# Layer 1's recurrence: TensorE in the order of the code, three items advanced stage by stage, state and systems stored compactly by head

## The chip, the cores and the metric

One core of one Trainium2 chip runs the whole program in one launch. The metric is device time in microseconds (us). Five engines work side by side, each through its own instructions in a fixed order: TensorE (PE; its weight loads are shown as PEld), VectorE (DVE), ScalarE (ACT), GpSimd (POOL), and SyncE (SP), which here only issues DMAs.

## The reference

One inference step of a two-layer trunk. Layer 0 is a gated delta rule, layer 1 is RWKV-7 time mixing; both run over 16 meta tokens and 1024 prompt tokens (one sequence) and over 8 decode sequences of 8 tokens. The change touches layer 1 alone. Its core, for 16 heads of width 64:

```python
def step(S, inp):
    r_t, k_t, v_t, d_t, kk_t, b_t = inp
    S = (S * d_t[:, :, None, :]
         + jnp.einsum('bhvk,bhk->bhv', S, -kk_t)[..., None] * b_t[:, :, None, :]
         + v_t[..., None] * k_t[:, :, None, :])
    return S, jnp.einsum('bhvk,bhk->bhv', S, r_t)
...
y = (y - mean) * lax.rsqrt(var + GN_EPS) * lnx_w.reshape(H, N) + lnx_b.reshape(H, N)
y = y + jnp.sum(r_h * k_h * r_k, -1, keepdims=True) * v_h
y = y.reshape(B, T, D) * jax.nn.silu(z)
return y @ w_o, S, xn[:, -1]
```

Everything is float32; the kernel computes the large dense products as sums of three products of split float32r parts.

## The kernel before, in words

The tokens lie in three segments (`SEGS`: 384, 384 and 336 columns). The first 64 columns are the 8 decode sequences, the rest the prompt. An item is a pair of heads `p` (8 of them) in a segment `s`: 24 items, each with six chunks `ci` of 64 tokens. The recurrence is evaluated in chunked form. A chunk's step needs the state `S` that the same pair left behind, so the six steps of an item, and the three items of a pair, are a chain; different pairs are independent.

For each item `rwkv_front` loads keys, decays and values and makes the decayed operands `AR` and `BK`, the score matrices `G` (matmuls `fG`), the transposed keys `BT` (`fBT`) and values `UV` (`fVT`) and the bonus term (`fbonus`, `rbv`); names with `f` in front are its PSUM tiles. `rwkv_step` does one chunk in a PSUM tile `rA` (`pA` in the code, one bank, three buffers). The two heads' state is kept as a block-diagonal 128x128 tile, so that one matmul serves both heads. In order: `AR` times state plus scores, a scaled copy `rX` on ACT for each head, the triangular system `rTT` times `rX`, a copy `UV` on ACT, `AR` times state again plus the scores of the outputs, `BT` times `UV`, the new state `rS` on DVE for each head, a copy `y` on ACT. `pre` is the decayed old state. `rwkv_finish` normalises `y` (`bnst`, `mv`, `grs`), transposes it (`zyT`) and gates it (`lz`, `yh`, `yl`). For segment 0 `rwkv_sample_read` and `rwkv_sample_write` handle the decode states (`drsr`, `drsw`, with masked operands `ue`).

Dense products run beside the recurrence: the gates of segments 1 and 2 (`zz`, 384 matmuls, weights `rwkv_w_rkvz`) and the output projection (`d`, 576 matmuls, weights `rwkv_w_o`), then the final norm (`finish`, `dfin`). A counter `tau` runs over the code that writes all this: item `n` starts its steps at `tau = 2n`, so three items are under way at once. A list scheduler with a model of times turns the code into the fixed order of every engine, TensorE's too.

Of the kernel before, what the change touches and what calls it, by code (L numbers as in the profile page):

```python
# [35 lines left out]
class Builder:  # L36
# [38 lines left out]
    def mm(self, out, lhsT, rhs, start=True, stop=True):  # L75
        self.nc.tensor.matmul(out, lhsT, rhs, start=start, stop=stop)  # L76

# [942 lines left out]
    def rwkv_gates(self, xa, s, pool, xb=None):  # L1020
# [3 lines left out]
        c0, n = SEGS[s]  # L1024
        for k in range(8):
# [5 lines left out]
            self.split(x, f[:, 0, k, 0:n], f[:, 1, k, 0:n], eng_lo="dve" if k % 2 else "pool")  # L1031
        xh, xl = ([f[:, x, k, 0:n] for k in range(8)] for x in (0, 1))
        for k in range(8):
            w = self.load_w(self.i["rwkv_w_rkvz"][0, 3][:, 128 * k:128 * k + 128])
            p = self.ps("d", 4, "z") if s == 0 else self.ps("z", 1, "z")
            c = 0
            for q in range(8):
                wh, wl = w[0][q // 4][:, q % 4], w[1][q // 4][:, q % 4]
                for l, r in ((wh, xh[q]), (wl, xh[q]), (wh, xl[q])):
                    self.mm(p[:, 0:n], l, r, start=c == 0, stop=c == 23)  # L1040
                    c += 1
            z = t(pool, [128, 384], "ev", 3) if s == 0 else t(pool, [128, 384], "zst", 2)
# [273 lines left out]
    def rwkv_front(self, p, s):  # L1316
        nc, t, ap, col = self.nc, self.t, self.ap, self.pcol
        P = Ctx()
        P.n = 8 * s + p
        NB = self.NB  # L1320
        pc = lambda n: col[n][:, p:p + 1]
        P.TT = t(ap, [128, 6, 64], "rTT", 3)
        nc.sync.dma_start(P.TT.rearrange("p c k -> p (c k)"), self.ttd[P.n])
# [6 lines left out]
        AR = P.AR = t(ap, [128, 6, 2, 64], "AR", NB)  # L1330
# [15 lines left out]
        bp = self.ps("f", 2, "bonus")  # L1346
        ph, pl = t(ap, [128, 384], "prh", 1, F32R), t(ap, [128, 384], "prl", 1, F32R)
        self.split(pr, ph, pl, "act", "pool")
        self.mm(bp[:, 0:384], self.bones, ph, start=True, stop=False)
        self.mm(bp[:, 0:384], self.bones, pl, start=False, stop=True)  # L1350
        bv = P.bv = t(ap, [128, 384], "rbv", NB + 1)
        nc.vector.tensor_tensor(bv, ld["v"], bp[:, 0:384], op=ALU.mult)

        G = P.G = t(ap, [128, 6, 2, 128], "G", NB)
        for c in (0, 3):
            for h in (0, 1):
                gp = self.ps("f", 2, "G")
                q = slice(64 * h, 64 * h + 64)
                for u in range(3):
                    self.mm(gp[:, 128 * u:128 * u + 128], flat(BK[q, c + u]), flat(AR[q, c + u]))  # L1360
                g3 = gp[:, 0:384].rearrange("p (q k) -> p q k", k=128)
                f = 0
                if s == 0 and c == 0:
                    nc.vector.tensor_tensor(G[:, 0, h, :], g3[:, 0, :], self.gms, op=ALU.mult)
                    f = 1
                nc.vector.tensor_tensor(G[:, c + f:c + 3, h, :], g3[:, f:3], self.gm.unsqueeze(1).broadcast_to([128, 3 - f, 128]),
                                        op=ALU.mult)
# [3 lines left out]
        for c in (0, 3):  # L1371
# [4 lines left out]
        vp = self.ps("f", 2, "VT")  # L1376
        for u in range(3):
            self.transpose(vp[:, 128 * u:128 * u + 128], ld["v"][:, 128 * u:128 * u + 128])
        for a in (0, 1):
            nc.scalar.copy(UV[0:64, a:6:2].rearrange("p c h k -> p c (h k)"),  # L1380
                           vp[64 * a:64 * a + 64, 0:384].rearrange("p (c k) -> p c k", k=128))
        return P

    def rwkv_step(self, p, s, P, ci):
        nc, t, ap = self.nc, self.t, self.ap
        AR, G, BT, UV, TT, DC = P.AR, P.G, P.BT, P.UV, P.TT, P.DC
        c = 6 * s + ci
        smp = c == 0
        if ci == 0:
            P.y = t(ap, [128, 3, 2, 64], "y", 4)  # L1390
        y = P.y[64 * (ci % 2):64 * (ci % 2) + 64, ci // 2]
        rk = self.rk2[:, 6 * P.n + ci:6 * P.n + ci + 1]
        hs = [slice(0, 64), slice(64, 128)]
        flat = lambda x: x.rearrange("p a b -> p (a b)")
        xs = P.xs if smp else None
        S = self.S[p]
        pA = self.ps("r", 3, "A")

        if c > 1:
            self.mm(pA[0:64, 0:128], AR[:, ci, 0], flat(S), start=True, stop=False)  # L1400
        for h in (0, 1):
            self.mm(pA[0:64, 64 * h:64 * h + 64], G[:, ci, h, 0:64], UV[:, ci, h, :], start=c <= 1, stop=c <= 1 or h == 1)
        X = self.X[P.n % len(self.X)]
        for h in (0, 1):
            src = pA[0:64, 64 * h:64 * h + 64]
            if smp:
                nc.vector.tensor_tensor(X[hs[h], h, :], src, xs[0:64, hs[h]], op=ALU.add)
                nc.vector.tensor_scalar(X[hs[h], h, :], X[hs[h], h, :], rk[hs[h]], None, op0=ALU.mult)
            else:
                self.act(X[hs[h], h, :], src, AF.Identity, scale=rk[hs[h]])  # L1410
        if c > 1:
            pre = t(ap, [128, 128], "pre", 3)
            self.act(pre, flat(S), AF.Identity, scale=DC[:, ci:ci + 1])
        self.mm(pA[64:128, 128:256], TT[:, ci, :], flat(X))
        self.act(UV[64:128, ci].rearrange("p h k -> p (h k)"), pA[64:128, 128:256], AF.Identity, scale=-1.0)
        if c > 1:
            self.mm(pA[64:128, 256:384], AR[:, ci, 1], flat(S), start=True, stop=False)
        for h in (0, 1):
            self.mm(pA[64:128, 256 + 64 * h:320 + 64 * h], G[:, ci, h, 64:128], UV[:, ci, h, :], start=c <= 1,
                    stop=c <= 1 or h == 1)  # L1420
        py = pA[64:128, 256:384]
        if smp:
            nc.vector.tensor_tensor(flat(y), py, xs[64:128, :], op=ALU.add)
            return
        for h in (0, 1):
            self.mm(pA[hs[h], 384:448], BT[:, ci, hs[h]], UV[:, ci, h, :])
        for h in (0, 1):
            dS = pA[hs[h], 384:448]
            if c == 1:
                nc.vector.tensor_scalar(S[hs[h], h, :], dS, DC[hs[h], ci:ci + 1], None, op0=ALU.mult)  # L1430
            else:
                nc.vector.scalar_tensor_tensor(S[hs[h], h, :], dS, DC[hs[h], ci:ci + 1], pre[hs[h], hs[h]], op0=ALU.mult,  # L1432
                                               op1=ALU.add)
        nc.scalar.copy(flat(y), py)

    def rwkv_finish(self, p, s, P):
# [8 lines left out]
        y6 = y.rearrange("p c h k -> p (c h) k")  # L1445
# [6 lines left out]
        yp = self.ps("z", 1, "yT")  # L1452
# [3 lines left out]
        for q in range(3):  # L1456
            self.transpose(yp[:, 128 * q:128 * q + 128], y[:, q].rearrange("p h k -> p (h k)"))
        t1 = t(ap, [128, 384], "t1", 1)
        nc.vector.scalar_tensor_tensor(t1[:, 0:n], yp[:, 0:n], self.lnw[:, p:p + 1], P.bv[:, 0:n], op0=ALU.mult, op1=ALU.add)
        nc.vector.scalar_tensor_tensor(zg[:, 0:n], t1[:, 0:n], self.lnb[:, p:p + 1], zg[:, 0:n], op0=ALU.add, op1=ALU.mult)  # L1460
        yh, yl = t(self.fin, [128, 384], "yh", 8, F32R), t(self.fin, [128, 384], "yl", 8, F32R)
        self.split(zg[:, 0:n], yh[:, 0:n], yl[:, 0:n])
        if s == 2:
            sp = self.ps("z", 1, "sT")
            S = self.S[p]
            self.transpose(sp[:, 0:128], S.rearrange("p h k -> p (h k)"))
            so = t(ap, [128, 64], "so", 1)
            for h in (0, 1):
                q = slice(64 * h, 64 * h + 64)
                nc.scalar.copy(so[q], sp[q, q])  # L1470
            nc.sync.dma_start(self.o["p_rwkv"][0, 0, 2 * p:2 * p + 2].rearrange("h v k -> (h v) k"), so)
        return yh, yl

    def rwkv_sample_read(self, p, P, AR):

        nc, t, ap = self.nc, self.t, self.ap
        st = self.i["state_rwkv"][0].rearrange("(g u) h v k -> u v g h k", u=2)
        sn = t(self.fin, [128, 4, 2, 64], "sn", 1)
        for u in (0, 1):
            for g in range(4):  # L1480
                nc.sync.dma_start(sn[64 * u:64 * u + 64, g], st[u][:, g, 2 * p:2 * p + 2, :])
        sp = self.ps("d", 2, "sn")
# [3 lines left out]
        nc.scalar.copy(P.Sb.rearrange("p b k -> p (b k)"), sp)  # L1486
        rp = self.ps("d", 2, "rsr")
# [6 lines left out]
        self.transpose(rp[:, 128:256], q.rearrange("p x b r -> p (x b r)"))  # L1494
        xs = t(ap, [128, 128], "xss", 3)
        nc.vector.tensor_copy(xs, rp[:, 128:256])
        return xs

    def rwkv_sample_write(self, p, P, BT, UV, DC):
        nc, t, ap = self.nc, self.t, self.ap  # L1500
        ps = self.ps("d", 2, "rsw")
        for h in (0, 1):
            ue = t(self.fin, [128, 8, 64], "ue", 2)
# [5 lines left out]
        nc.vector.tensor_tensor(P.Sb, P.Sb, DC[:, 6:14].unsqueeze(2).broadcast_to([128, 8, 64]), op=ALU.mult)  # L1509
        op = self.ps("d", 2, "sbT")  # L1510
# [10 lines left out]
    def project_out(self, s, yo, pairs, x2):  # L1521

        nc, t, i = self.nc, self.t, self.i
        c0, n = SEGS[s]
        for ft in range(8):
            w = self.load_w(i["rwkv_w_o"][0][128 * pairs[0]:128 * pairs[-1] + 128, ft * 128:(ft + 1) * 128], len(pairs))
            if len(x2) < 8:
                x = t(self.fin2, [128, 384], "x2", 8)
                nc.sync.dma_start(x[:, 0:n], self.x1T[ft][:, c0:c0 + n])
                x2.append(x)  # L1530
            x = x2[ft]
# [3 lines left out]
            for k, q in enumerate(pairs):  # L1535
                wh, wl = w[0][k // 4][:, k % 4, :], w[1][k // 4][:, k % 4, :]
# [245 lines left out]
```

## Time and profile before

| | |
|---|---|
| three runs | 2451.74, 2457.27, 2458.03 us; median 2457.27 |
| profiled execution | 2460.66 us, span 2458.9 us |
| TensorE busy | 2273.3 us, 92% of the span |
| DVE, ACT, POOL busy | 66%, 56%, 43% |
| first and last matmul of the recurrence | 1872.8 us and 2418.2 us |

The profile is of one execution. Busy time of TensorE is the union of its matmuls from start to modelled end, and since matmuls are pipelined, a busy TensorE can hold stalls of up to about one matmul's length. Every float32 matmul stands in the trace as two rows here, called passes below; float32r products and transposes are one row each.

### The profile page before, as it was taken

Reading aid. Unit: us, or ns where it says so; the run is one execution under the profiler, and the core shown is the slowest. Engines: PE = TensorE matmul, PEld = TensorE weight load, DVE = VectorE, ACT = ScalarE, POOL = GpSimd, SP = SyncE. Lnnn points to the kernel's source line nnn. Section 1 sums busy time; section 2 is a strip of 40 time slices with the busy share of each in tenths; the row PEclk is TensorE's granted clock in tenths of the full one; section 3 lists DMA queues with packets and bytes.
Section 4 is the critical chain, followed back from the end, with each engine's and each line's share of the span. In section 5 each row is a group of like instructions: output and inputs, shape, how many; then the busy total and the mean of one; then the engine's idle time right before and its main releaser. Section 6 shows DMA issues by size and latency. Waiting matters only on the chain. (4 is left out here: it accounts for less than half of the span.)

```text
span 2458.9 us, 52218 instructions
## 1 busy us (share of the span) xinstructions
PE 2273.3 (92%) x18377; PEld 2041.3 (83%) x18377; DVE 1632.2 (66%) x4338; ACT 1370.2 (56%) x3817; POOL 1061.1 (43%) x1454
## 2 busy tenths in 40 slices
PE   6989999999999999999999999998879998998996
PEld 5888989898988989889899998777768877877875
DVE  6868676876768586843358344798865586576554
ACT  5445546555555564664336466564434666677673
POOL 3435343433444343451315235343456554554543
PEclk9989999999999999999999999989989998999998
DMA  3323333333332424261531556667665552342331
GB/s 109 106 69 99 85 107 84 102 86 85 87 102 66 117 79 109 71 204 57 145 100 42 163 176 159 173 186 194 152 193 166 141 150 80 94 148 78 106 102 54
DMA packets 471935, 284.61 MB, mean 116 GB/s; under 512 B 187481, under 2 KB 457050, under 8 KB 471674
## 3 DMA queue, kind: packets, MB, share of 16 engines
q1 hardware_dynamic: 471674, 281.29, 40.6%
q8 instruction: 145, 2.38, 0.4%
q14 instruction: 116, 0.95, 0.1%
HBM read 200.00 MB, written 81.17 MB: 114 GB/s over the span
## 5 line engine op out<-in xcount | busy, mean ns | idle before, releaser
L86 POOL TENSOR_TENSOR wlo<-wraw,whi 128x512 fp32r<-128x512 f32 x260 | 346.2, 1335 | 358.8 <-ACT whi L82 327.7
L82 ACT CAST whi<-wraw 128x512 fp32r<-128x512 f32 x260 | 159.9, 617 | 152.2 <-PE dq L76 50.6
L76 PE MATMUL d<-xc,whi 128*128 128x384 f32 (+3 forms) x846 | 237.9, 338 | 2.1 <-ACT ev L1145 2.1
L406 DVE SCALAR_TENSOR_TENSOR cvy<-raw,cw,cvy 128x408 f32<-128x408 f32 (+2 forms) x288 | 178.1, 631 | 16.6 <-ACT cvy L62 14.8
L439 DVE TENSOR_TENSOR invtmp<-invA,invT 72x31 f32<-72x31 f32 (+31 forms) x403 | 165.7, 411 | 16.7 <-POOL invT L434 6.0
L441 DVE TENSOR_TENSOR invT<-invT,invtmp 72x31 f32<-72x31 f32 (+31 forms) x403 | 169.1, 420 | 6.4
L76 PEld LDWEIGHTS d<-xc,whi 128*128 128x128 f32 (+1 forms) x846 | 154.5, 190 | 9.8 <-issue 5.3
L76 PE MATMUL dz<-xc,whi 128*128 128x384 f32 (+1 forms) x480 | 149.6, 343 | 0.0
L76 PE MATMUL dv<-xc,whi 128*128 128x384 f32 (+1 forms) x480 | 146.7, 335 | 0.0
L76 PE MATMUL d<-xa,whi 128*128 128x384 f32 (+3 forms) x450 | 140.0, 344 | 4.2 <-ACT xa L82 2.5
L76 PE MATMUL dz<-xa,whi 128*128 128x384 f32 (+1 forms) x416 | 137.3, 352 | 3.6 <-ACT whi L82 3.0
L76 PE MATMUL d<-xc,wlo 128*128 128x384 f32 (+2 forms) x396 | 130.6, 340 | 0.0
L76 PE MATMUL rA<-rS,AR 128*64 128x128 f32 x512 | 108.1, 295 | 18.2 <-ACT UV L62 7.5
L855 POOL TENSOR_SCALAR Sb<-Sb,eglb 128x128 f32<-128x128 f32 x128 | 81.1, 651 | 86.2 <-DMA Sb<-in_state_gdn 37.7
L76 PE MATMUL rA<-UV,G 128*64 128x64 f32 x1152 | 114.8, 225 | 0.8 <-ACT UV L1380 0.8
L76 PEld LDWEIGHTS rA<-UV,G 128*64 128x64 f32 x1152 | 104.0, 140 | 5.4 <-issue 2.3
L76 PE MATMUL dv<-xa,whi 128*128 128x384 f32 (+1 forms) x288 | 99.9, 347 | 0.1
L62 ACT ACTIVATE rX<-rA,rk 64x64 f32<-64x64 f32 x272 | 83.6, 307 | 20.6 <-PE rA L76 14.9
L1432 DVE SCALAR_TENSOR_TENSOR rS<-rA,DC,pre 64x64 f32<-64x64 f32 x256 | 72.2, 282 | 32.6 <-PE rA L76 27.7
L76 PEld LDWEIGHTS d<-xa,whi 128*128 128x128 f32 (+1 forms) x450 | 84.2, 192 | 9.4 <-ACT xa L82 2.8
L76 PE MATMUL dz<-xa,wlo 128*128 128x384 f32 (+1 forms) x256 | 89.8, 351 | 2.1 <-POOL wlo L86 2.1
L76 PEld LDWEIGHTS dz<-xc,whi 128*128 128x128 f32 x480 | 89.8, 192 | 0.8
(505 smaller groups left out, 7412.4 us busy)
## 6 DMA issues: line engine op xcount, KB each, us to landing
wraw<-in_gdn_w_in SPq DMA_DIRECT2D x96, 256.0 KB
wraw<-in_rwkv_w_rkvz SPq DMA_DIRECT2D x96, 256.0 KB
Sb<-in_state_gdn SPq DMA_DIRECT2D x64, 256.0 KB
wraw<-in_rwkv_w_o SPq DMA_DIRECT2D x48, 256.0 KB
E<-drow SPq DMA_DIRECT2D x24, 384.0 KB
attn<-drow SPq DMA_DIRECT2D x24, 384.0 KB
wraw<-in_gdn_w_out SPq DMA_DIRECT2D x36, 256.0 KB
out_s_gdn<-Sb SPq DMA_DIRECT2D x32, 256.0 KB
```

What stands on the lines that cost most here:

```text
L62: return self.nc.scalar.activation(out, in_, func, bias=bias, scale=scale, **kw)
L76: self.nc.tensor.matmul(out, lhsT, rhs, start=start, stop=stop)
L82: nc.scalar.copy(hi, x)
L86: e.tensor_tensor(lo, x, hi.bitcast(F32), op=ALU.subtract)
L406: nc.vector.scalar_tensor_tensor(y[:, 0:wd], raw[:, k:k + wd], cw[k], y[:, 0:wd], op0=ALU.mult, op1=ALU.add)
L439: nc.vector.tensor_tensor(tmp, A[:, j, j + 1:32].unsqueeze(2).broadcast_to([nb, n, m]), Tv[:, j, 0:m].unsqueeze(1).broadcast_to([nb, n, m] ...
L441: nc.vector.tensor_tensor(Tv[:, j + 1:32, 0:m], Tv[:, j + 1:32, 0:m], tmp, op=ALU.subtract)
L855: nc.gpsimd.tensor_scalar(Sb[:, u], Sb[:, u], self.eglb[:, hv, 4 * g + u:4 * g + u + 1], None, op0=ALU.mult)
L1432: nc.vector.scalar_tensor_tensor(S[hs[h], h, :], dS, DC[hs[h], ci:ci + 1], pre[hs[h], hs[h]], op0=ALU.mult, op1=ALU.add)
```

## The change

State and systems: `S` becomes 128x64 (each head's 64x64 block on its own partitions), `X` becomes 128x64, and the systems `TT` are read into a tile that has zeros where the other head's rows would be. Products with the state are then one matmul for each head, 64 rows by 64 columns; all outputs of a step lie at the partitions of their head. One ACT copy makes `X` for both heads, one DVE instruction the new state.

Order: TensorE's instructions now keep the order in which the code writes them; the other engines stay with the list scheduler. The step is cut in five methods, and in each `tau` all items do one stage before any does the next. Into three gaps of each `tau` the code puts a part of the coming item's front, a piece of six dense matmuls (two pieces where two dense jobs are open, three before the first step), and pieces of the decode work. The front of an item is written one `tau` earlier. Weights of the dense products are fetched one tile ahead. The output projection runs in halves of four pairs in every segment. The outputs of a step are written after the new state. `ue` has one buffer instead of two.

```diff
+    def mmx(self, out, lhsT, rhs, start=False):
+        self.nc.tensor.matmul(out, lhsT, rhs, start=start, stop=True, skip_group_check=True)
...
+        P.parts = [[sc(0, 0)], [sc(0, 1), bonus], [values], [lambda: keys(0), sc(3, 0)], [system, sc(3, 1)], [lambda: keys(3)]]
...
+    def step_solve(self, P, ci):
+        if c > 1:
+            for h in (0, 1):
+                self.mmx(pA[hs[h], 0:64], AR[hs[h], ci, 0], S[hs[h]], True)
+            for h in (0, 1):
+                self.mmx(pA[hs[h], 256:320], AR[hs[h], ci, 1], S[hs[h]])
+    def step_scores(self, P, ci):
+        for h in (0, 1):
+            self.mmx(pA[hs[h], 0:64], G[:, ci, h, 0:64], UV[:, ci, h, :], c <= 1)
...
+        with self.tc.high_priority():
+            self.act(X, pA[:, 0:64], AF.Identity, scale=rk)
+        if c > 1:
+            P.pre = t(ap, [128, 64], "pre", 3)
+            self.act(P.pre, S, AF.Identity, scale=P.DC[:, ci:ci + 1])
+    def step_inner(self, P, ci):
+        for h in (0, 1):
+            self.mmx(pA[64:128, 128 + 64 * h:192 + 64 * h], P.TT[:, h, ci], P.X)
+        with self.tc.high_priority():
+            self.act(UV[64:128, ci].rearrange("p h k -> p (h k)"), pA[64:128, 128:256], AF.Identity, scale=-1.0)
+    def step_state(self, P, ci):
         for h in (0, 1):
+            self.mmx(pA[hs[h], 384:448], BT[:, ci, hs[h]], UV[:, ci, h, :])
+        with self.tc.high_priority():
...
+                nc.vector.scalar_tensor_tensor(S, pA[:, 384:448], DC[:, ci:ci + 1], P.pre, op0=ALU.mult, op1=ALU.add)
+    def step_outputs(self, P, ci):
         for h in (0, 1):
+            self.mmx(pA[64 * h:64 * h + 64, 256:320], G[:, ci, h, 64:128], UV[:, ci, h, :])
...
+            nc.scalar.copy(P.y[:, ci], pA[:, 256:320])
...
-        for q in range(3):
-            self.transpose(yp[:, 128 * q:128 * q + 128], y[:, q].rearrange("p h k -> p (h k)"))
+        yield
+        yp = self.ps("f", 2, "yT")
+        for q in range(6):
+            for h in (0, 64):
+                self.mm(yp[h:h + 64, 64 * q:64 * q + 64], y[h:h + 64, q], self.ident[h:h + 64, h:h + 64])
...
-            ue = t(self.fin, [128, 8, 64], "ue", 2)
+            ue = t(self.fin, [128, 8, 64], "ue", 1)
...
+        with tc.manual_schedule(engines={mybir.EngineType.PE}):
+            self.wave(xa, stay, last, pool)
...
+        for tau in range(-3, 54):
+            if (tau + 3) % 2 == 0 and (tau + 3) // 2 < 24:
+                s, p = divmod((tau + 3) // 2, 8)
+                P[8 * s + p] = self.rwkv_front(p, s)
+            m = (tau + 2) // 2
+            parts = P[m].parts[3 * (tau % 2):3 * (tau % 2) + 3] if 0 <= m < 24 else [[], [], []]
+            items = [(P[n], tau - 2 * n) for n in range(max(0, (tau - 4) // 2), min(24, tau // 2 + 1)) if 0 <= tau - 2 * n < 6]
+            stages = (self.step_solve, self.step_scores), (self.step_inner,), (self.step_state, self.step_outputs)
+            for g in range(3):
+                for f in stages[g]:
+                    for x in items:
+                        f(*x)
+                for f in parts[g]:
+                    f()
...
+                fill(3 if tau < 0 else 1 + (len(todo) > 1))
```

Three places show how the orders differ. On TensorE before, in the middle of the recurrence: `rA_27586` and `rA_27604` are the PSUM tiles of two items' steps.

```order
L76 MATMUL rA_27604<-rS_4107_23024,AR_27069 64x128
L76 MATMUL rA_27604<-UV_4115_23032,G_27091 64x64 x2
L76 MATMUL fbonus_27656<-prh_27657,bones_23011 128x384
L76 MATMUL fbonus_27656<-prl_27658,bones_23011 128x384
L76 MATMUL rA_27586<-rS_4106_23023,AR_26762 64x128
L76 MATMUL rA_27586<-UV_4114_23031,G_26784 64x64 x2
L76 MATMUL rA_27586<-UV_4114_23031,BT_26805 64x64 x2
L76 MATMUL rA_27604<-rX_4111_23028,rTT_27048 64x128
```

One item's products stand between the other's, each item at another point of its step. The same engine in the changed kernel, at the end of one `tau`: the three items' products for the state (`BT`), then the three for the outputs (`G`). What an instruction waits for stands behind it.

```order
L80 MATMUL rA_26753<-UV_4110_23027,BT_25600 64x64 [waits Activation_49]
L80 MATMUL rA_26753<-UV_4110_23027,BT_25600 64x64
L80 MATMUL rA_26759<-UV_4111_23028,BT_25962 64x64 [waits Activation_49]
L80 MATMUL rA_26759<-UV_4111_23028,BT_25962 64x64
L80 MATMUL rA_26766<-UV_4112_23029,BT_26294 64x64 [waits Activation_49]
L80 MATMUL rA_26766<-UV_4112_23029,BT_26294 64x64
L80 MATMUL rA_26753<-UV_4110_23027,G_25599 64x64 [waits DVE_49]
L80 MATMUL rA_26753<-UV_4110_23027,G_25599 64x64
L80 MATMUL rA_26759<-UV_4111_23028,G_25961 64x64 [waits DVE_49]
L80 MATMUL rA_26759<-UV_4111_23028,G_25961 64x64
L80 MATMUL rA_26766<-UV_4112_23029,G_26293 64x64 [waits DVE_49]
L80 MATMUL rA_26766<-UV_4112_23029,G_26293 64x64
```

The outputs moved behind the state's products, and each item's outputs now wait for DVE, which reads the same PSUM tile for the new state. Before, the outputs came first.

On ACT, before: the two copies `rX` of an item, and what stands behind them until the next copy `UV`.

```order
L62 ACTIVATE rX_4111_23028<-rA_27604,rk_10_97 64x64 [waits PE_49]
L62 ACTIVATE rX_4111_23028<-rA_27604,rk_10_97 64x64
L62 ACTIVATE fDp_27923<-fldcs_27911 128x384 [waits DMAHW0_49,Pool_49]
L82 CAST yh_27275<-lz_27242 128x384 [waits DVE_49]
L62 ACTIVATE UV_4115_23032<-rA_27604 64x128 [waits PE_49]
```

On ACT in the changed kernel, in the `tau` shown above: the three items' copies `X` and `UV`.

```order
L62 ACTIVATE X_26754<-rA_26753,rk_10_97 128x64 [waits PE_49]
L62 ACTIVATE X_26760<-rA_26759,rk_10_97 128x64 [waits PE_49,Activation_49]
L86 CAST yh_26749<-lz_26414 128x384 [waits DVE_49]
L62 ACTIVATE k_4950_26857<-flda_26838,omka_23017,pcol_385 128x384 [waits DMAHW7_49]
L62 ACTIVATE X_26767<-rA_26766,rk_10_97 128x64 [waits PE_49,Activation_49]
L62 ACTIVATE UV_4110_23027<-rA_26753 64x128 [waits PE_49]
L62 ACTIVATE UV_4111_23028<-rA_26759 64x128 [waits PE_49]
L62 ACTIVATE UV_4112_23029<-rA_26766 64x128 [waits PE_49]
```

Six copies became three, and the third `X` stands behind two ACT instructions of other work.

On DVE, before, around the new state of the two items above.

```order
L1352 TENSOR_TENSOR rbv_27663<-fldv_27632,fbonus_27656 128x384 [waits DMAHW6_49,PE_49]
L1448 BN_AGGR mv_27552<-bnst_27551 128x2 [waits DVE_49]
L1565 SCALAR_TENSOR_TENSOR f2k_27906<-dfin_27881,frs_27895,fw_24737 128x512 [waits DMAHW7_49,DMAHW6_49]
L1448 BN_AGGR mv_27552<-bnst_27551 128x2 [waits DVE_49]
L1432 SCALAR_TENSOR_TENSOR rS_4106_23023<-rA_27586,DC_26760,pre_27592 64x64 [waits PE_49]
L1432 SCALAR_TENSOR_TENSOR rS_4106_23023<-rA_27586,DC_26760,pre_27592 64x64
L1432 SCALAR_TENSOR_TENSOR rS_4107_23024<-rA_27604,DC_27067,pre_27610 64x64 [waits PE_49,Activation_49]
L1432 SCALAR_TENSOR_TENSOR rS_4107_23024<-rA_27604,DC_27067,pre_27610 64x64
```

On DVE in the changed kernel, in the same `tau` as above.

```order
L1352 TENSOR_TENSOR k_4950_26857<-k_4950_26857,fldk_26836 128x384 [waits DMAHW0_49,Activation_49]
L106 SCALAR_TENSOR_TENSOR grs_26724<-gn_t_26726,grs_26724 128x6 [waits DVE_49]
L1356 TENSOR_TENSOR BK_26861<-k_4950_26857,fiD_26847 128x6x64 [waits DVE_49]
L1361 SCALAR_TENSOR_TENSOR pr_26864<-fldr_26840,pcol_385,k_4950_26857 128x384
L1384 TENSOR_TENSOR G_26607<-fG_26801,gm_22991 128x3x128 [waits PE_49]
L1370 TENSOR_TENSOR rbv_26606<-fldv_26578,fbonus_26806 128x384 [waits PE_49]
L1469 SCALAR_TENSOR_TENSOR rS_4102_23019<-rA_26753,DC_25579,pre_26775 128x64 [waits PE_49,Activation_49]
L1469 SCALAR_TENSOR_TENSOR rS_4103_23020<-rA_26759,DC_25941,pre_26780 128x64 [waits PE_49,Activation_49]
L1469 SCALAR_TENSOR_TENSOR rS_4104_23021<-rA_26766,DC_26273,pre_26785 128x64 [waits PE_49,Activation_49]
```

The new states went from two instructions for each item to one, three in a row, behind the front's work for the next item.

More of the change, by code (lines that the diff above doesn't have):

```diff
@@ L1354, in rwkv_front, with bonus @@
-        G = P.G = t(ap, [128, 6, 2, 128], "G", NB)
[L1355 to L1367, printed above, removed]
+        def bonus():
+            bp = self.ps("f", 2, "bonus")
+            self.mm(bp[:, 0:384], self.bones, ph, start=True, stop=False)
+            self.mm(bp[:, 0:384], self.bones, pl, start=False, stop=True)
+            nc.vector.tensor_tensor(bv, ld["v"], bp[:, 0:384], op=ALU.mult)
@@ L1421, in rwkv_step @@
[L1421 to L1433, printed above, removed]
@@ L1754, with wave_out @@
+    def wave_out(self, P, n, x2, todo):
+        s, p = divmod(n, 8)
+        next(P[n].done, None)
+        half = lambda a, b: [P[8 * s + q].out for q in range(a, b)]
+        if p % 4 == 3:
+            x2.setdefault(s, [])
+            todo.append(self.project_out(s, half(p - 3, p + 1), range(p - 3, p + 1), x2[s]))
+        if p == 7:
+            todo.append(self.finish(s, x2[s]))
 _INS = ["x_prompt", "x_sample", "state_gdn", "state_gdn_conv", "state_rwkv", "state_rwkv_shift", "meta_tokens", "norm_w",
```

245 lines of the change are left out of this document (134 added, 111 removed).

## The prediction

> **What bounds the kernel now.** I read the page first, then the stretch from the recurrence's first matmul (1872.8 us) to its last (2418.2 us), then who waits there, then the timeline of TensorE for the price of a pass.
>
> ```profile
> PE 2273.3 (92%) x18377; PEld 2041.3 (83%) x18377; DVE 1632.2 (66%) x4338; ACT 1370.2 (56%) x3817; POOL 1061.1 (43%) x1454
> core 0: us, PE busy (x) PEld busy (x) DVE busy (x) ACT busy (x) POOL busy (x), PEclk, DMA share, GB/s
> 1872.80:2418.20 545.40, 511.00 (x4488) 425.46 (x4488) 348.59 (x1061) 367.45 (x1031) 291.98 (x327) 0.97 0.39 113
> ```
>
> In 545.4 us TensorE is idle for 545.4 - 511.0 = 34.4 us only. DVE is busy for 64%, ACT for 67%, POOL for 54%. The stretch is bound by what TensorE has to issue, so each pass saved there is time saved, until a wait takes its place.
>
> ```profile
> start us, us, engine line op out<-in xcount [idle before <-releaser]
> 2103.65 0.43 PE L76 MATMUL rA<-rS,AR 128*64 128x128 f32 x2
> 2103.92 0.22 PE L76 MATMUL rA<-UV,G 128*64 128x64 f32 x1
> 2103.92 0.27 PE L76 MATMUL rA<-UV,BT 128*64 128x64 f32 x1
> 2103.97 0.22 PE L76 MATMUL rA<-UV,G 128*64 128x64 f32 x1
> 2104.03 0.22 PE L76 MATMUL rA<-UV,BT 128*64 128x64 f32 x1
> 2104.03 0.28 PE L76 MATMUL rA<-UV,G 128*64 128x64 f32 x2
> 2104.15 0.28 PE L76 MATMUL rA<-UV,BT 128*64 128x64 f32 x2
> 2104.26 0.39 PE L76 MATMUL rA<-rX,rTT 128*64 128x128 f32 x2
> 2104.58 0.93 PE L76 MATMUL fG<-AR,BK 64*128 64x128 f32 x6
> 2105.44 0.43 PE L76 MATMUL rA<-rS,AR 128*64 128x128 f32 x2
> ...
> 2011.27 1.11 PE L76 MATMUL drsr<-AR,Sb 64*64 64x16 f32 x32
> 2012.31 0.43 PE L76 MATMUL rA<-rS,AR 128*64 128x128 f32 x2
> ```
> ```profile
> L76 PE MATMUL rA<-UV,G x1152: 219/222/366, 1872.8 to 2418.1; 128*64 128x64 f32 x192
> L76 PE MATMUL rA<-UV,BT x544: 222/222/368, 1892.7 to 2418.2; 128*64 128x64 f32 x182
> L76 PE MATMUL rA<-rS,AR x512: 272/275/476, 1895.6 to 2417.8; 128*64 128x128 f32 x171
> L76 PE MATMUL rA<-rX,rTT x288: 272/273/477, 1880.8 to 2417.0; 128*64 128x128 f32 x144
> L76 PE MATMUL drsr<-AR,Sb x256: 206/206/286, 1843.4 to 2012.2; 64*64 64x16 f32 x128
> ```
>
> The first fence is the timeline (start, length of the group), the second the tile views (shortest, median and longest pass in ns). A group's length less one pass's, divided by the rest of the count, is the spacing. Passes of 128 columns: (0.39 - 0.273) / 1 = 0.11 us. Passes of 64 columns to the same partitions: (0.28 - 0.222) / 1 = 0.058 us. The step's eight passes of `G` and `BT` take 0.34 us (2103.92 to 2104.26): a pass that writes partitions 64 to 127 and one that writes 0 to 63 start together at 2103.92, and four passes have gone by 2104.03, 0.029 us each. The `drsr` products, 64 rows by 64 columns for either head, also run at (1.11 - 0.206) / 31 = 0.029 us. After a change of shape the first pass comes late: `rTT` to `fG` takes 0.32 us, 0.10 more than its two passes.
>
> **The change part by part.** *Passes of the recurrence.* Before, a step has six passes of 128 columns (0.66 us), eight at 0.34 us together and four scores at 0.058 (0.23 us): 1.23 us, over 144 steps and less what the 16 first steps lack, 169 us. After, a step has 20 passes that alternate between the two heads' partitions and four (`step_inner`) that all write 64 to 127: 20 x 0.029 + 4 x 0.058 = 0.81 us, in all 112 us. **-57 us.** The alternation of whole heads (two passes, then two) is that of `drsr` and of `G` and `BT`; without any overlap it would be 24 x 0.058 = 1.39 us a step.
>
> *Transposes of `y`*: 72 transposes of one pass (0.11 us) become 288 matmuls of two passes at 0.029: 8 against 17 us, **+9**.
>
> *Changes of shape*: counted over the stretch in the two orders, 451 before and 491 after, at 0.10 us for the late pass and about 0.05 for the one behind it: **+6** (0 to 10).
>
> *Outputs behind the state.* This is the new wait.
>
> ```profile
> L1432 DVE SCALAR_TENSOR_TENSOR rS<-rA,DC,pre 64x64 f32<-64x64 f32 x256 | 72.2, 282 | 32.6 <-PE rA L76 27.7 <-ACT y L1434 0.5 <-ACT yh L82 0.4
> ACT y L1434 <- DVE rS L1432: 35.1, 43, 3.1
> ```
>
> In the kernel before, the copy `y` on ACT waits for the new state on DVE (35.1 us, 43 times) though both only read the tile; that wait lay on ACT, beside TensorE's work. Now TensorE itself stands in it: an item's outputs wait until DVE has read the tile, and what is queued behind is the whole coming gap. From the first `BT` pass: 0.06 + 0.22 us to the end of an item's passes, three DVE instructions of 0.28, and the last item's four passes, 0.12: 1.25 us, where 24 passes unhindered take 24 x 0.029 = 0.70. That is 0.55 us at least, and DVE reaches each of the three through a semaphore, for which I add 0.1. DVE is 64% busy with instructions of 0.33 us on average (348.59 / 1061); another 0.16 us for finding it occupied gives 0.8 us. There are 47 such rounds: **+38** (20 to 60; 30 with DVE always free, 47 x 0.65).
>
> *`ue` with one buffer.*
>
> ```profile
> L1504 POOL TENSOR_TENSOR ue<-UV,bmask 128x512 f32<-128x512 f32 x8 | 10.8, 1354 | 8.4 <-ACT UV L62 8.4
> L1504 DVE TENSOR_TENSOR ue<-UV,bmask 128x512 f32<-128x512 f32 x8 | 6.8, 845 | 1.9 <-ACT UV L62 1.8
> L76 PE MATMUL drsw<-ue,BT 128*64 128x512 f32 x32 | 9.7, 609 | 0.0
> ```
>
> The second head's `ue` (0.845 us on DVE) can begin only when the first head's matmul (0.61 us) has read the one buffer, and TensorE waits in order: 1.3 us, 8 times, **+10** (5 to 12).
>
> *The other waits.* TensorE can no longer go round a late operand. What hides the copies is a front part and a dense piece in each gap.
>
> ```profile
> L62 ACT ACTIVATE rX<-rA,rk 64x64 f32<-64x64 f32 x272 | 83.6, 307 | 20.6 <-PE rA L76 14.9
> 2200.54 0.44 PE L76 MATMUL d<-yh,whi 128*128 128x384 f32 x1
> 2200.82 0.34 PE L76 MATMUL d<-yl,whi 128*128 128x384 f32 x1
> ...
> 2201.71 0.34 PE L76 MATMUL d<-yh,whi 128*128 128x384 f32 x1
> ```
>
> Three copies `X` in a row take 3 x 0.31 us, and the pass before them 0.22, 1.2 us; a gap holds six `fG` passes (0.86 us, above) and, where there is dense work, six dense matmuls (2200.54 to 2201.71, 1.17 us): 2.0 us, covered. Counting the pieces that the code hands out (41 of the gates and 80 of the projection left after the first step, one or two a gap), about 12 of 52 rounds have none. There the third gap (a transposed group and the next `solve`) is short by some 0.5 us, and the second by about as much: 12 x 1.1 = 13 us. Late operands of other kinds I put at 9 us. So the idle 34 us of before become 22: **-12** (-25 to +45).
>
> *Start and tail.* 138 instead of 96 gate matmuls now stand ahead of the first step; at 0.18 us (five matmuls from 2200.82 to 2201.71) that is 7 us less in the stretch, of which the start pays back half: **-3** (-8 to +4). The projection's last half and the final norm keep their 41 us (2418.2 to 2458.9).
>
> *Other engines.* 272 copies `rX` become 136 (-42 us on ACT), 256 states 128 (-36 us on DVE); the projection in halves adds 16 DVE additions. Neither engine is the bound; at nothing on the path. SP issues two DMAs for a system instead of one: nothing, as the code writes them a round ahead of their first use.
>
> Sum: -57 + 9 + 6 + 38 + 10 - 12 - 3 = -9 us on the profiled execution's 2460.66 us (span 2458.9). That execution is 3.4 us above the median of the three runs; the same -9 on the median 2457.27 gives **2448 us**. What a measurement here can tell from no change is about 0.3%, 7.4 us.
>
> On the pairs that share all rows and differ in their output partitions (scores, state, outputs): the row above has them start together. The Trainium skill (TensorE: Matmul & The Clock Gate, Part 3: Packing small matmuls — row/col tiling) says that a weight load overlaps a matmul in flight only where the two use different row groups; by that rule these passes would not overlap, and the sum would be that of the second rival. The trace at 2103.92 speaks against it.
>
> **The rivals.** *A. ScalarE and VectorE become what TensorE waits for (slower).* Both keep an order laid out by a model, and TensorE now cannot go round them.
>
> ```profile
> L62 ACT ACTIVATE k<-flda,omka,pcol 128x384 f32<-128x384 f32 x20 | 14.1, 704 | 6.8 <-DMA flda<-ad 6.6
> L82 ACT CAST yh<-lz 128x384 fp32r<-128x384 f32 x16 | 8.1, 509 | 3.7 <-DVE lz L1460 3.3 <-PE d L76 0.3
> L1345 DVE SCALAR_TENSOR_TENSOR pr<-fldr,pcol,k 128x384 f32<-128x384 f32 x21 | 14.9, 711 | 1.7 <-POOL prl L86 1.6
> L1340 DVE TENSOR_TENSOR BK<-k,fiD 128x384 f32<-128x384 f32 x21 | 14.4, 685 | 3.7 <-PE fBT L73 3.2 <-ACT fiD L62 0.4
> ```
>
> In the changed order ACT has `yh` and `k` (0.51 + 0.70 us) ahead of the third `X`, and DVE has `BK`, `pr`, one `G` and `rbv` ahead of the new states. In every second round that delays `step_inner` by about 0.8 us and the states by as much: 24 x 1.6 = 38 us over the forecast, at 2486 us. For it: ACT and DVE are at two thirds before, and the stretch would get shorter. Against: in rounds with dense pieces 1.17 us for each gap cover it. It decides from 0.17 us a round (9 / 52).
>
> *B. The column pairs don't overlap (slower).* 1696 passes of scores, state and outputs at 0.058 instead of 0.029 us: +49 us, 2497 us. Against it stands the row at 2103.92.
>
> *C. The waits fit in the gaps.* DVE takes the states at once (30 instead of 38 us) and only 10 of the 34 idle us stay: another -20 us, 2428 us. For it: in the stretch before, no wait of TensorE's own on the recurrence's operands sums to much.
>
> ```profile
> PE rA L76 <- ACT UV L62: 7.5, 11, 1.5
> PE rA L76 <- DVE rS L1432: 6.6, 15, 0.8
> 2060.00:2100.00 40.00, 34.97 (x235) 27.47 (x234) 20.70 (x58) 21.66 (x61) 13.81 (x19) 0.74 0.21 65
> ```
>
> *D. The clock.* From 2060 to 2100 us the granted clock is 0.74. More short waits could bring another such stretch; each loses about 0.26 x 40 = 10 us, two of them put the result at 2468 us.
>
> **How the numbers follow.** Forecast (2438 to 2460 us) 0.40; A 0.30; B 0.04; C 0.22; D 0.04. Faster by over 0.3% (below 2449.9) are C and a little over half of the forecast: 0.44; within 0.3% the rest of the forecast: 0.18; slower A, B and D: 0.38. The unknown costs are the wait for DVE (20 to 60) and the other waits; the range, 2418 to 2488 us, takes in C with the least of both and A, and leaves out B and the joint extremes. The forecast's own range is 2438 to 2460 us.
>
> **What would show it.** Right: `rA` passes of `BT` and `G` in threes, a spacing of 0.029 us in the timeline; about 0.7 to 0.9 us between the last `BT` and the last `G` start of a round; waits "PE rA <- DVE rS" near 30 to 40 us; the stretch from first to last `rA` near 536 us. Wrong: spacing of 0.058 us (B); waits of `rA` on ACT `X` or DVE `G` of over 20 us (A); a stretch under 520 us (C); a granted clock under 0.95 in it (D).

## The result: slower by 1.3%, where 0.4% faster was forecast

| | before | changed |
|---|---|---|
| median | 2455.02 us (2451.74 to 2458.03, 4 runs) | 2486.28 us (2484.87 to 2493.25, 4 runs) |
| profiled execution, span | 2460.66, 2458.9 us | 2484.87, 2483.2 us |
| first to last matmul of the recurrence | 1872.8 to 2418.2 = 545.4 us | 1880.6 to 2443.9 = 563.3 us |

The ratio is 1.0127 (95% interval 1.0101 to 1.0152), against a forecast of 2448 us in a range of 2418 to 2488. The span grew by 24.3 us: the recurrence starts 7.8 us later, takes 17.9 us more, and what follows it takes 1.4 us less (40.7 against 39.3). Of the later start, 3.2 us lie ahead of the first gate matmul (1824.9 and 1828.1 us), in code that the change leaves alone. One of the six runs of experiment 9 took 3018.1 us at a granted clock of 0.65; the ratio given there leaves it out, the median of the six does not.

The page's first part, and the row of that stretch (columns as in the prediction):

```profile
PE 2275.2 (92%) x19737; PEld 2038.0 (82%) x19737; DVE 1600.7 (64%) x4193; ACT 1293.6 (52%) x3673; POOL 1069.5 (43%) x1454
1880.60:2443.90 563.30, 505.26 (x5782) 414.94 (x5781) 316.98 (x928) 288.01 (x884) 293.88 (x323) 0.94 0.37 108
```

ScalarE lost 79 us of work in the stretch (367.45 to 288.01) and VectorE 32 (348.59 to 316.98), and it bought nothing: TensorE is the bound. Its own busy time fell by 5.7 us although 1294 passes were added, and its idle time rose from 34.4 to 58.0 us. The granted clock fell from 0.97 to 0.94: by its records TensorE ran at half speed for 27.3 us of the stretch before, for 68.3 us after.

The chain of waits on TensorE, from 1880 to 2440 us (what waited, for whom: us in all, times, longest):

```profile
PE rA L80 <- DVE rS L1469: 22.9, 47, 2.2
PE dfin L73 <- DVE f2k L1620: 11.0, 4, 4.1
PE drsw L76 <- DVE ue L1554: 10.7, 8, 2.6
PE d L76 <- POOL yl L90: 3.4, 2, 2.3
PE fbonus L76 <- DVE G L1384: 3.2, 2, 2.0
PE rA L80 <- ACT X L62: 2.3, 5, 0.9
```

The first and the third were in the forecast, at 38 and 10 us. The second was not: the final norm's transposes `dfin` now stand in the recurrence in the order of the code, and those of a tile wait until VectorE has read the one before. The fourth is a projection waiting for the low part of its operand, which GpSimd makes. The last two are what rival A lived on; together they are 5.5 us.

One of the longest waits for `rS`, in the timeline of TensorE and then of VectorE:

```profile
2198.11 0.57 PE L80 MATMUL rA<-UV,BT 128*64 128x64 f32 x12
2200.77 0.91 PE L80 MATMUL rA<-UV,G 128*64 128x64 f32 x12 [2.09 <-DVE rS L1469]
2201.61 0.90 PE L73 MATMUL fVT<-ident,fldv 128*128 128x128 f32 x3
```
```profile
2198.34 0.55 DVE L1384 TENSOR_TENSOR G<-fG,gm 128x384 f32<-128x384 f32 x1
2198.81 0.71 DVE L1356 TENSOR_TENSOR BK<-k,fiD 128x384 f32<-128x384 f32 x1
2199.45 0.60 DVE L1361 SCALAR_TENSOR_TENSOR pr<-fldr,pcol,k 128x384 f32<-128x384 f32 x1
2199.98 0.54 DVE L1370 TENSOR_TENSOR rbv<-fldv,fbonus 128x384 f32<-128x384 f32 x1
2200.44 0.66 DVE L1469 SCALAR_TENSOR_TENSOR rS<-rA,DC,pre 128x64 f32<-128x64 f32 x3
```

Twelve passes of `BT` take 0.57 us, (0.57 - 0.222) / 11 = 0.032 us each: the overlap of the column pairs is there, and rival B is out. Then TensorE stands still for 2.09 us, since VectorE has four instructions of the next item's front ahead of the new states. And the three transposes behind take 0.90 us, where three such take 0.55 us at full speed (shown below).

That half speed can be followed in windows laid on the grid of the clock's records, 3.41 us wide:

```profile
2176.26:2179.67 3.41, 0.00 (x0) 0.00 (x0) 1.53 (x7) 0.93 (x4) 0.55 (x1) 1.00 0.32 103
2179.67:2183.08 3.41, 3.35 (x32) 2.92 (x32) 1.38 (x4) 1.38 (x4) 0.66 (x1) 0.50 0.52 132
2183.08:2186.50 3.42, 1.93 (x23) 1.48 (x21) 2.61 (x6) 1.51 (x5) 2.46 (x5) 1.00 0.03 8
2186.50:2189.91 3.41, 3.09 (x20) 2.79 (x20) 1.60 (x5) 1.72 (x6) 0.00 (x0) 0.50 0.66 224
2196.74:2200.15 3.41, 1.94 (x21) 1.43 (x20) 3.34 (x8) 1.64 (x6) 2.01 (x2) 1.00 0.55 156
2200.15:2203.56 3.41, 2.37 (x27) 1.85 (x29) 1.52 (x8) 2.71 (x10) 1.00 (x1) 0.50 0.49 154
2213.80:2217.22 3.42, 3.42 (x57) 3.19 (x56) 2.02 (x8) 1.10 (x3) 2.80 (x3) 0.50 0.00 0
```

Behind the window and its width stands TensorE's busy time; the third number from the end is the clock. The windows in which TensorE was busy for 0.00, 1.93 and 1.94 of 3.41 us at full clock are each followed by one at half clock, and the last stay at half speed goes on for five windows (2200.1 to 2217.2 us). No dense matmul stands in these five windows.

### The profile page after: what moved, and what is told of

Its sections match the earlier page's. It is cut to its first block, busy times and chain, and to the rows that moved or that the text cites. A ratio compares the mean times of both kernels' runs of the same rounds, so it can differ in the third digit from the quotient of the medians.

```text
span 2483.2 us, 54705 instructions
## 1 busy us (share of the span) xinstructions
PE 2275.2 (92%) x19737; PEld 2038.0 (82%) x19737; DVE 1600.7 (64%) x4193; ACT 1293.6 (52%) x3673; POOL 1069.5 (43%) x1454
## 5 line engine op out<-in xcount | busy, mean ns | idle before, releaser
L1384 DVE TENSOR_TENSOR G<-fG,gm 128x384 f32<-128x384 f32 (+1 forms) x96 | 50.8, 530 | 89.4 <-PE fG L76 89.3
L76 PE MATMUL zz<-xa,whi 128*128 128x384 f32 (+1 forms) x256 | 80.1, 364 | 15.0 <-DVE zst L1054 10.1
L76 PE MATMUL fG<-AR,BK 64*128 64x128 f32 x576 | 93.6, 298 | 0.0
L76 PEld LDWEIGHTS dz<-xa,whi 128*128 128x128 f32 x416 | 81.9, 199 | 9.1 <-ACT whi L86 7.5
L76 PEld LDWEIGHTS dv<-xc,whi 128*128 128x128 f32 x480 | 88.5, 188 | 0.5 <-issue 0.4
```

## The experiments

The theory: TensorE's work did shrink as worked out, and four things used up what was gained: the outputs behind VectorE, the one `ue`, the norm's tiles, and half speed in rounds without dense work. The rival that runs through all tests: these waits are only places where a chain of an item's stages shows, and whatever is removed comes back elsewhere. Unless said otherwise each kernel is the changed one with one edit. The chips of these runs took 2462 us for the kernel before, so kernels are compared by their ratios to it, and a difference in ratio is turned into us with some 2455 us. The changed kernel counts as 1.0127; on the chip of experiments 7, 9 and 10 it was 1.0151, so 6 us between two sets of runs are no finding.

**1. Outputs ahead of the state.**

```diff
-stages = ..., (self.step_state, self.step_outputs)
+stages = ..., (self.step_outputs, self.step_state, self.step_copy)   # step_copy: the copy y alone
```

> One part undone: the outputs' matmuls stand ahead of the state's again, and the copy y on ACT behind the new state on DVE; all else as in the changed kernel (2486.3 us). Theory: TensorE's wait between the last BT and the first G (28.7 us by spacing, 23.3 us as listed for rS) goes, and with it half-speed stretches that begin in it (68 us at half speed in the recurrence, 27 before): 2446 to 2461 us, half-speed time under 50 us. Rival 1 (the wait is displaced: the same item's next solve waits for the state instead, since its chain sets the length of a round): 2478 us or more. Rival 2 (the clock has a cause of its own): 2457 to 2466 us, with half-speed time still near 68 us.

Measured: 2468.17 us, ratio 1.0014 (0.9994 to 1.0035): 0.0113 less, 28 us. By that ratio it is some 2458 us on the chip of the forecast, where the theory and rival 2 overlap. The stretch is 538.7 us.

```profile
1896.30:2435.00 538.70, 494.00 (x5782) 409.44 (x5781) 320.17 (x927) 282.33 (x884) 289.88 (x323) 0.93 0.39 112
PE rA L80 <- ACT y L1485: 9.1, 7, 3.3
PE rA L80 <- DVE rS L1469: 1.9, 1, 1.9
```

The wait for `rS` went from 22.9 to 1.9 us, and only a part of it came back, on the copy `y`. But the time at half speed stayed, at 71.7 us. So the wait costs 25 to 28 us, within the forecast's 20 to 60, and it is not by itself what sets the clock: there the theory was wrong, and the half-speed time came as rival 2 had it. Whether the clock has a cause of its own is what experiments 4 and 5 ask.

**2. Two `ue`.**

```diff
-ue = t(self.fin, [128, 8, 64], "ue", 1)
+ue = t(self.fin, [128, 8, 64], "ue", 2)      # and X in 3 buffers instead of 4
```

> One part undone: ue has two buffers again (X has three instead of four to make room); all else as in the changed kernel (2486.3 us). Theory: the second drsw matmul of a decode write no longer waits for VectorE (10.7 us listed, 16.4 us by spacing, in eight places): 2472 to 2478 us. Rival 1 (waits are displaced, since another chain sets the round): 2483 us or more.

Measured: 2485.0 us, ratio 1.0087 (1.0061 to 1.0114), 10 us less. The time itself lies where the rival put it, but on a chip 7 us slower for the kernel before; by the ratio it is some 2476 us, as the theory had it. The interval overlaps that of the changed kernel (1.0101 to 1.0152), so the runs alone hardly separate the two. The stretch of the profiled execution fell by 11.3 us to 552.0, and the wait of `drsw` is gone from the list, which now begins:

```profile
PE rA L80 <- DVE rS L1469: 28.5, 46, 2.3
PE dfin L73 <- DVE f2k L1620: 11.1, 4, 4.1
```

The wait for `rS` reads 28.5 us here and 22.9 in the changed kernel, so a part of what was removed may have come back in it.

**3. The norm's tiles apart.**

```diff
                     nc.sync.dma_start(yp[...], y[0:nr])
             yield
+            for _ in range(3 if s < 2 else 0):
+                yield
```

> One thing added: in segments 0 and 1 the final norm's three tiles stand three empty pieces apart in TensorE's order, so that the transposes dfin of a tile find the PSUM of the tile before it read; all else as in the changed kernel (2486.3 us). Theory: the wait of dfin for f2k (11.0 us listed, 8.5 by spacing, four places) goes: 2475 to 2481 us, and fewer half-speed pieces from 2174 to 2200 us. Rival 1 (waits are displaced; the empty pieces take cover away elsewhere): 2484 us or more.

Measured: 2479.85 us, ratio 1.0074 (1.0048 to 1.0099), 13 us less, as the theory had it; the stretch is 551.1 us. `dfin` is gone from the list, and a wait of 4.5 us in one place is new, of the transposes `fyT` for `y` on GpSimd.

**4. Dense pieces spread.**

```diff
-fill(3 if tau < 0 else 1 + (len(todo) > 1))
+fill(3 if tau < 0 else 1 if g < 2 else tau < 16 or len(todo) > 1)
```

> One thing changed: from the seventeenth round on the dense pieces are handed out one to each of a round's first two gaps (in the third gap only when two dense jobs are open), so that no round is without a piece; all else as in the changed kernel (2486.3 us). Theory (half speed begins in rounds that wait without dense work): half-speed time in the recurrence falls from 68 to under 40 us, the wait before the outputs stays near 25 us, 2466 to 2480 us. Rival 1 (a piece in each gap hides no more than two in half of them): 2483 to 2490 us. Rival 2 (the clock has a cause of its own): half-speed time near 68 us.

Measured: 2461.84 us, ratio 0.9999 (0.9983 to 1.0015): 31 us less, more than expected, from the order of the dense matmuls alone.

```profile
1888.70:2420.50 531.80, 488.75 (x5758) 399.26 (x5757) 312.38 (x926) 286.06 (x882) 289.48 (x321) 0.97 0.39 113
PE rA L80 <- DVE rS L1469: 24.3, 48, 1.8
```

The wait for the state is as long as ever, and half speed fell to 30.7 us, 38 less than in the changed kernel. In all twelve runs the mean clock of the whole program was 0.967 to 0.972, in the four of the changed kernel 0.958 to 0.961. If half the issue is lost at half speed (an estimate from the granted 0.50), some 19 of the 31 us are the clock. The rest fits the waits: TensorE's idle time in the stretch fell from 58.0 to 43.0 us, and in the lists `dfin` waits for 7.1 us instead of 11.0 and `drsw` for 8.0 instead of 10.7. The two shares were not separated by a run of their own, and 24 matmuls of the projection moved behind the stretch.

**5. Work added to keep TensorE busy.** In the 16 rounds with no dense job open:

```diff
+if f == self.step_outputs and not todo and tau > 12 and items:
+    w = self.ps("d", 2, "warm")
+    for q in range(8):
+        self.transpose(w[:, 0:128], self.ident)
```

> Work added: between the state's and the outputs' products of each of the 16 rounds that have no dense job open, eight transposes of a constant into a spare PSUM buffer that nobody reads (0.11 us each, 14 us of TensorE's issue in all); all else as in the changed kernel (2486.3 us). Theory (half speed follows rounds in which TensorE is busy for too small a part): the wait for VectorE there takes up some 10 of the 14 us, the half-speed time falls from 68 to under 45 us: 2470 to 2484 us. Rival (half speed has a cause of its own): half-speed time 60 us or more, 2487 to 2500 us.

Measured: 2485.8 us, ratio 1.0105 (1.008 to 1.013).

```profile
1890.70:2442.00 551.30, 504.43 (x5908) 415.01 (x5909) 317.29 (x928) 289.24 (x884) 293.48 (x323) 0.98 0.38 110
PE rA L80 <- DVE rS L1469: 16.6, 38, 1.2
```

With 14 us of useless work more, the stretch is 12 us shorter, and half speed fell from 68.3 to 27.3 us. That is one execution of each, but in all six runs the mean clock of the whole program was 0.964 to 0.966, above each of the changed kernel's four (0.958 to 0.961). So most of the half-speed time has no cause of its own: it follows how busy TensorE is. By the ratio the kernel is not measurably slower for that work (1.0105 against 1.0127 and, in another set of runs, 1.0151); the absolute time missed the 2470 to 2484 us by 2, on a chip 7 us slower for the kernel before.

**6. The list scheduler for TensorE.** `manual_schedule` taken away.

> One part undone: TensorE is given to the list scheduler again like the other engines; layout, stages and the code's order as in the changed kernel (2486.3 us). Theory (the layout saves TensorE some 46 us and the fixed order loses more than that in waits that it cannot go round): faster than before, ratio 0.975 to 0.995, half-speed time under 45 us. Rival (the order is not at fault: the outputs behind the state and one ue cost the same in any order): ratio 1.005 or more.

Measured: 2470.32 us, ratio 1.0042 (1.0018 to 1.0065): the theory's 0.975 to 0.995 fell. The rival's 1.005 lies in the interval, but its reason, the same waits in any order, does not hold either:

```profile
1871.70:2425.10 553.40, 525.90 (x5884) 426.82 (x5883) 326.72 (x937) 302.20 (x896) 305.03 (x333) 0.97 0.39 114
PE rA L80 <- ACT UV L62: 11.1, 9, 2.8
PE rA L80 <- DVE rS L1469: 7.1, 9, 1.9
PE rA L80 <- ACT y L1480: 4.4, 3, 2.8
```

The waits for `ue` and `f2k` are gone, that for `rS` is a third, half speed is down to 34.1 us. The stretch is 9.9 us shorter and begins 38.5 us after the first gate matmul instead of 52.5, so some 24 us were won where the theory wanted 43 at least. The waits don't hold the rest: TensorE is idle for 553.4 - 525.9 = 27.5 us, less than the 34.4 before. What grew is the number of changes of shape: counted over the passes of the stretch they are 451 before, 491 in the changed kernel, 714 here. With the compact state a step needs one shape more (64 rows by 64 columns). Experiment 7 asks what a change costs.

**7. The price of a change of shape**, on one set of runs with the changed kernel as it is.

```diff
-stages = (self.step_solve, self.step_scores), ...
+stages = (lambda P, ci: (self.step_solve(P, ci), self.step_scores(P, ci)),), ...
```

> The changed kernel as it is, to have its time and trace on the same chip as the next three. Both theories: ratio 1.010 to 1.015, half-speed time in the recurrence 55 to 80 us.

> One order changed: in a round's first stage the products of an item with the state (64 rows by 64 columns) and its scores (128 by 64) stand together, item after item, where the changed kernel has all items' state products and then all scores; the same passes, some 185 more changes of shape on TensorE. Theory (a change of shape costs TensorE 0.10 to 0.15 us wherever it stands; this is where the list order lost what it saved in waits, with 714 changes against 491): 18 to 28 us over the changed kernel, ratio 1.018 to 1.025. Rival (the late first pass is hidden by waits for ScalarE that follow anyway): ratio within 0.003 of the changed kernel's.

Measured: the changed kernel 2498.23 us, ratio 1.0151 (1.012 to 1.0181); by item 2515.2 us, 1.0212 (1.0181 to 1.0243).

```profile
1884.60:2455.60 571.00, 518.58 (x5780) 427.24 (x5781) 316.94 (x928) 288.27 (x884) 294.12 (x323) 0.91 0.36 106
1892.60:2472.20 579.60, 534.87 (x5780) 433.73 (x5781) 317.20 (x928) 294.37 (x884) 290.18 (x323) 0.93 0.36 105
```

There are 156 changes more (647 in the stretch, not the 185 more that I had put), and 17.0 us by the medians: 0.11 us each, with the number of passes equal. The runs of a kernel here lie up to 9 us apart, so the price is good to some 0.03 us. (The two rows differ by 8.6 us only: the execution of the first was at half speed for 102 us, that of the second for 85, and half of that difference makes up the rest.) The waits that follow don't hide it. In the list order 223 changes more are thus some 24 us, an estimate from this price, and about what kept it from the time expected. The first row has a second message: the same program spent 102 us at half speed here, on another chip, and 68 in the execution shown above, so this loss is not the same in every run.

**8. The four edits together** (1 to 4; the norm's tiles one empty piece apart).

> The four edits of the first runs together (outputs ahead of the state, two ue, the norm's tiles one empty piece apart, dense pieces one to a gap), all else as in the changed kernel. Alone they took 28, 10, 13 and 31 us off it by their ratios to the kernel before (1.0014, 1.0087, 1.0074, 0.9999 against 1.0127). Theory (each removes a wait or half speed of its own): little is counted twice but the norm's wait, which the spreading partly holds too: ratio 0.965 to 0.980. Rival (beneath these waits lies a chain of an item's stages that sets the round): the sum shrinks to that of the best alone and a little more, ratio 0.985 to 0.998.

Measured: 2438.4 us, ratio 0.9917 (0.9886 to 0.9947): faster than before, but in the rival's range.

```profile
1883.20:2385.90 502.70, 470.05 (x5752) 390.86 (x5751) 318.92 (x924) 279.89 (x881) 288.71 (x320) 0.97 0.41 119
PE rA L80 <- ACT y L1485: 13.2, 23, 0.9
PE fVT L73 <- DVE G L1384: 5.7, 8, 1.8
PE rA L80 <- DVE rS L1469: 4.0, 4, 1.6
```

Alone the edits shortened the stretch by 24.6, 11.3, 12.2 and 31.5 us, 79.6 in all; together by 60.6, of which some 4 us are dense work that moved behind the stretch (43.3 us follow it, 39.3 in the changed kernel). Two reasons can be seen why they don't add up: the spread pieces alone had already shortened the waits of `dfin` and `drsw`, and a new wait appears, for the copy `y`, which holds the PSUM buffer that the next step needs. That copy waits in its turn for VectorE, in the waits of ScalarE:

```profile
ACT y L1485 <- DVE rS L1469: 55.9, 37, 3.0
```

**9. A fourth bank.** The kernel of the four edits, with one more:

```diff
-pA = P.pA = self.ps("r", 3, "A")
+self.turn = getattr(self, "turn", 0) + 1
+pA = P.pA = self.ps(*(("z", 1) if 6 * P.n + ci > 60 and self.turn % 4 == 0 else ("r", 3)), "A")
```

> The four edits together, and once the gates' PSUM bank is free every fourth step takes it for rA (from the eleventh item on), so that a new step need not wait for the copy y of the same item's last one. Theory (that wait, 13.2 us in 23 places in the run of the four edits, is what replaced the wait for the state): 6 to 12 us less, ratio 0.986 to 0.990. Rival (the step waits for the new state a moment later anyway): ratio 0.990 to 0.994.

Measured: 2422.56 us, ratio 0.9844 (0.9806 to 0.9882), the best of all: 1.6% under the kernel before, and more than the theory's 6 to 12 us under the run of the four edits (0.0073, 18 us; the two intervals do not touch).

```profile
1883.70:2375.00 491.30, 465.32 (x5752) 388.89 (x5751) 320.65 (x924) 277.89 (x881) 289.93 (x320) 0.97 0.41 122
PE rA L80 <- ACT y L1486: 3.1, 6, 0.9
```

The recurrence's last step stands in the fourth bank here, in the tile `zA`, and the row runs to its last matmul. With the same 5752 passes the wait for `y` fell from 13.2 to 3.1 us and the stretch by 11.4. So that wait was for a buffer and not for a chain of stages. What the 26.0 us still idle would yield was not tried.

**10. Another cure for the outputs**: the kernel of the four edits, but with the state first, then the front's part, then the outputs.

```diff
-(self.step_outputs, self.step_state, self.step_copy)
+(self.step_state,)
 ...
+for f in (self.step_outputs, self.step_copy) if g == 2 else ():     # behind the front's part
+    for x in items:
+        f(*x)
```

> The edits two ue, norm apart and pieces spread, with another cure for the outputs: the state's products come first again, then the front's part of the third gap, and the outputs and their copy after that. Theory (what counts is that TensorE has something of its own to do while VectorE reads the bank; the part has 0.3 to 0.4 us of the 0.55 to 0.8): a little of the wait stays, 8 to 15 us of it; ratio 0.990 to 0.998, a little above the run of the four edits. Rival (the state early is worth more than the wait costs, since the next solve needs it): ratio under 0.990.

Measured: 2446.4 us, ratio 0.9942 (0.9919 to 0.9965), as the theory had it, and not to be told from the run of the four edits; that the state early is worth more than the wait (under 0.990) is out.

```profile
PE rA L80 <- DVE rS L1469: 13.5, 17, 2.3
PE rA L80 <- ACT y L1485: 7.7, 9, 2.2
```

## Why the prediction was wrong

- *Passes, transposes and shapes* (-57, +9, +6, together -42): held as far as it can be seen. The spacing is 0.032 us (2198.11) where 0.029 was put, a change of shape costs 0.11 us (experiment 7), and with the four edits the stretch is 502.7 us, 42.7 below before. That agreement is partly luck, since other waits differ too, and 7 us of gate matmuls and some 4 us of the projection moved out of the stretch. One reading is off: (0.39 - 0.273) is 0.117 us for a pass of 128 columns, not 0.11, which by the prediction's own count makes the saving some 6 us larger.
- *Outputs behind the state* (+38, 20 to 60): right in kind and 10 to 13 us too high. The wait is 22.9 us as listed, in the 47 places that were forecast, and undoing it is worth 24.6 us of the stretch and 28 by ratio.
- *`ue`* (+10): right; 10.7 as listed, 11.3 of the stretch and 10 by ratio when undone.
- *The other waits* (-12): **this is the step that failed.** With -42, the 7 us of gate matmuls moved ahead, and 24.6 and 11.3 for the two waits, a stretch that grew by 17.9 us leaves 17.9 + 42 + 7 - 24.6 - 11.3 = +31 for all else, if the -42 held in full, where -12 was forecast. Two things make up some 32 us of it, so nothing is left of the fall in idle time that was forecast. The norm's transposes in the order of the code: 11.0 us, 12.2 when undone; I had counted its pieces as cover for the recurrence, and not asked whom they wait for themselves. And half speed: 41 us more of it, some 20 us of lost issue (half of the 41, an estimate). I had found the 12 rounds without dense work and priced them at 1.1 us each by the copies that they don't cover, but not by the clock.
- *Start and tail* (-3): right. The first gate matmul to the first step grew by 4.6 us (47.9 to 52.5), where half of 7 was put, and the tail fell by 1.4: -7 + 4.6 - 1.4 = -3.8. The 3.2 us ahead of the gates come on top.
- *Rival A* gave the time that came, 2486 us, for a reason that did not come, so that agreement is luck: its waits on `X` and `G` are 5.5 us. VectorE's front work ahead of the states, which it spoke of, is in the wait for `rS`.
- *Rival D* named the mechanism (a clock under 0.95 in the stretch) and sized it at two stretches of 10 us, with a chance of 0.04. It was about that size, and came on top of the other waits and not in place of them. That waits of TensorE can cost some 20 us more in clock is what the sum lacked.

## What to carry to other kernels

When an engine's order is fixed, list for every instruction that is put into it whom it waits for itself, the fillers included; a filler with a wait is no cover. Spread independent work so that no 3 or 4 us of TensorE stand thin, since a thin round is paid for twice, once by waiting and once by the clock. And count the changes of matmul shape in the order: with small operands they cost as much as four overlapping passes each.

## What had not been expected of the hardware

*The clock.* In the changed kernel's stretch, ten windows at full clock were followed by half clock. The share of the 3.41 us in which TensorE was busy was 0.00 to 0.72 in them, and under 0.6 in eight of the ten; of the windows that kept the clock, the thinnest had 0.46 and the next 0.59. This is no sharp limit: in the kernel before, a window of 0.55 kept the clock and two of 0.57 lost it, and in the repeated run of the changed kernel (experiment 7) one of 0.93 lost it. The Trainium skill (TensorE: Matmul & The Clock Gate, Part 1: The HAM clock gate) puts the half rate after at least one idle window of about 3.4 us; the rows above agree on the grid and on the half, but the windows before 2186.50 and 2200.15 were busy for 1.93 and 1.94 us, so here a window need not be idle. Coming back took one to five windows, and the last one was busy for a share of 0.90 or more each time.

*Changes of shape.* 0.11 us each in place, measured with equal passes (experiment 7). The Trainium skill (TensorEngine Tiling (Array Packing), Tiling Modes: Key Properties) says that a change of tiling mode drains TensorE and gives no price; this is one.

For comparison with the half-speed rows, three transposes at full speed take 0.55 us, and 24 passes with the state, the change of shape behind them included, 2198.70 - 2197.91 = 0.79 us or 0.033 each, in the timeline of the run of the four edits:

```profile
2196.68 0.55 PE L73 MATMUL fBT<-ident,BK 128*128 128x128 f32 x3
2197.16 0.91 PE L76 MATMUL fyT<-ident,y 64*64 64x64 f32 x24
2197.91 0.87 PE L80 MATMUL rA<-rS,AR 64*64 64x64 f32 x24
2198.70 0.57 PE L80 MATMUL rA<-UV,G 128*64 128x64 f32 x12
```
